# A recurrence with running maximum on one core: five steps of the last group, the start constants and the last store moved

## The chip, the core and the metric

The kernel runs on one core of a Trainium2 chip. The metric is device time in microseconds (us). Three timed runs of the kernel before took 290.93, 292.04 and 292.12 us (median 292.04). A further execution was profiled; it took 291.05 us, of which 289.3 us lie between its first and its last instruction (the span). Times in a trace are counted from the start of that span.

The engines are called as in the profile: PE (TensorE; PEld are its weight loads), DVE (VectorE), ACT (ScalarE), POOL (GpSimd) and SP (SyncE, which here only issues DMAs). A `q` behind a name (`POOLq`, `SPq`) marks what an engine's sequencer does, such as issuing a DMA or waiting.

## What is computed

For each of 16 batches and 256 channels a weighted mean runs over 2048 steps, with a numerator `aa`, a denominator `bb` and a running exponent `pp`:

```python
for t in range(seq_len):
    kk, vv = k[b, t, :], v[b, t, :]
    ww = u + kk
    qq = np.maximum(pp, ww)
    e1, e2 = np.exp(pp - qq), np.exp(ww - qq)
    output[b, t, :] = (e1 * aa + e2 * vv) / (e1 * bb + e2 + 1e-08)
    ww = pp - w + kk
    qq = np.maximum(ww, kk)
    e1, e2 = np.exp(ww - qq), np.exp(kk - qq)
    aa = e1 * aa + e2 * vv
    bb = e1 * bb + e2
    pp = qq
```

`k`, `v` and the output are 16 x 2048 x 256 in float32; `w` and `u` have 256 values each.

## The kernel before

Time is cut into 16 groups of 128 steps (`c` = 0 to 15), each of two halves of 64 steps, and the batches into 4 sets of four. A pair `n` = 4c + p (0 to 63) is one group for one set of batches: a tile of 128 steps x 4 batches x 256 channels for `k`, one for `v`, one for the output.

Each pair goes through these steps. Their short names are those of the plan in the code, and are used in the text:

- LK, LV load `k` and `v`, by SP for the first three pairs and by POOL after that (L108, L111, L115). RK rounds `k` for PE (`kr`, L194, DVE or POOL). CV casts `v` to bfloat16 (`vb`, L214, DVE for the first ten pairs).
- R and L put `u`, `w` and running sums of `k` into one of two PSUM tiles X0, X1 on PE (L201, L207), X takes the exponentials on ACT into the ring `EZR` (L210), and TV multiplies by `v` on DVE (L219). `u` and `w` reach PE through the tile WU, made by two operations on DVE (L175, L176) from the row tile WUf, which is cleared (L124) and then filled by two small DMAs (L122: `u` issued by POOL, `w` by ACT).
- S sums over the steps of the pair into the PSUM tile TOT on PE (L245).
- DEN forms the denominator in X0 or X1 on PE (L322), LN takes its logarithm on ACT (`rd<-X`, L330), INV takes exp of minus that on ACT (`rd<-rd`, L338). NUM forms the numerator on PE (L322, into the one tile `num`, or into X for the odd pairs of the last eight), MUL multiplies the two on DVE (`ot`, L350). There are two `rd` and eight `ot` buffers.
- ST stores the output by SP (L363 the first two batches; L356 a piece of 64 steps of the others). SQ stores the last piece: for pairs 52 to 63 by POOL (L356), before that by SP. For pair 63 INV and MUL are done in two halves.

Between the groups the state is carried on. After the last pair of group c: CS copies TOT to SBUF (DVE, L251), TU turns it on PE (L258), SL takes logarithms (ACT, L262), FR and OF make frames and offsets (DVE, L267 to L275), SW the weights from them (ACT, L281), CH runs two scans (DVE, L285, L288), SS spreads the result (DVE, L295), TK turns it back on PE (L302), BK copies it to the tile `cb` (DVE, L306). DEN and NUM of pairs 4c to 4c+3 read `cb` of group c, so the last four pairs, 60 to 63, need TK 15 and BK 15.

The order is written by a planner. Every step gets a place, a number in units of pairs, from the table P; steps are taken in order of place as soon as the steps that they follow and the buffers that they take are there, and each engine executes its instructions in that order. A table AT can set the place of a single step by name; it is empty before. The program ends (L480) when SP has waited for every store, each engine has drained, and a barrier led by POOL is through.

Ahead of the planned steps stands a start: memsets on DVE (WUf first), 26 multiplications by zero on PE that read the tile Z (L149), selects and iotas on POOL, and then on DVE nine memsets of state tiles (L231 to L236). The step `mats` (four small multiplications on DVE that make Id, IdN, S and SN, L182) has a place of -9.17 and follows directly.

```python
    for j in range(2):
        K(DVE.memset(CB_of[j].bitcast(F32), 0.0))
        K(DVE.memset(U_of[j][:, FR, :, 0:1], -BIG))
...
    step("mats", P["mats"], make_matrices)
    step("wu", P["wu"], make_rows)
```

Of the kernel before, what the change touches and what calls it, by code (L numbers as in the profile page):

```python
# [7 lines left out]
F32 = mybir.dt.float32  # L8
# [3 lines left out]
ACT = mybir.ActivationFunctionType  # L12
# [3 lines left out]
def kernel(  # L16
# [9 lines left out]
    K = tc.keep_in_program_order  # L26
    PE, DVE, SC, POOL, SP = nc.tensor, nc.vector, nc.scalar, nc.gpsimd, nc.sync
# [5 lines left out]
    D = 2 * Dm  # L33
    NP = 4 * NST
# [10 lines left out]
    RS = 2.0 ** -20  # L45
    CAP = 54.0
    BIG = 1e30
# [14 lines left out]
         "Z0": {"L": 1, "S": 3, "DEN": 0, "NUM": 6, "TK": 47, "TU": 17, "R": 12},  # L62
         "Z": {"DEN": 0, "L": 1, "NUM": 0, "TK": 4, "S": 0, "TU": 1, "R": 0}}

    AT = {}

    consts = ctx.enter_context(tc.tile_pool(name="consts", bufs=1))
    kpool = ctx.enter_context(tc.tile_pool(name="kpool", bufs=NK))
# [3 lines left out]
    rpool = ctx.enter_context(tc.tile_pool(name="rpool", bufs=NRD))  # L72
# [14 lines left out]
    def matrix(name, dt):  # L87
        return consts.tile([128, 128], dt, tag=name, name=name)
# [10 lines left out]
    def how(n):  # L99
        return "D" if n < BYSP else FIRST[n] if n < len(FIRST) else PLAN[n % len(PLAN)]  # L100
# [4 lines left out]
    def load_k(n):  # L105
        if how(n) != "C":
            KR[n] = raw(opool, "ot") if n < BYSP else raw(kppool, "kf")
            K((SP if n < BYSP else POOL).dma_start(out=KR[n], in_=rows_of(k, n)))  # L108
        else:
            KR[n] = kpool.tile([128, 4, Dm], F32R, tag="kr", name="kr")  # L110
            K(POOL.dma_start(out=KR[n], in_=rows_of(k, n)))  # L111
# [6 lines left out]
    WUf = rpool.tile([128, 2, D], F32, tag="rd", name="WUf")[:, 0, 0:Dm]  # L118
# [2 lines left out]
    def row_wu(queue, x, g):  # L121
        K(queue.dma_start(out=WUf[g::32, :], in_=bass.AP(tensor=x.tensor, offset=x.offset, ap=[[0, 4], list(x.ap[0])])))  # L122

    K(DVE.memset(WUf, 0.0))  # L124
    load_k(0)
    row_wu(POOL, u, 1)
    row_wu(SC, w, 0)
# [50 lines left out]
    mats = {name: matrix(name, BF16) for name in ("Id", "IdN", "S", "SN")}  # L178
# [11 lines left out]
    X = [psx.tile([128, 2, D], F32, tag=f"X{a}", name=f"X{a}") for a in range(2)]  # L190
# [31 lines left out]
    AS, D1, L1, A0, FR, BC, A2 = range(7)  # L222
    U_of = [consts.tile([128, 7, 32, 3], F32, tag=f"U{j}", name=f"U{j}") for j in range(2)]
    G_of = [consts.tile([128, 3, 32, 3], F32, tag=f"G{j}", name=f"G{j}") for j in range(2)]
    TB_of = [consts.tile([128, 2, 32, 3], F32, tag=f"TB{j}", name=f"TB{j}") for j in range(2)]
    CB_of = [consts.tile([128, 4, 128], BF16, tag=f"CB{j}", name=f"CB{j}") for j in range(2)]
    AB = consts.tile([128, 2, 32, 3], F32, tag="AB", name="AB")
    st = {}

    for j in range(2):  # L230
        K(DVE.memset(CB_of[j].bitcast(F32), 0.0))  # L231
        K(DVE.memset(U_of[j][:, FR, :, 0:1], -BIG))
        K(DVE.memset(G_of[j][:, :, :, 0:1], 0.0))
    K(DVE.memset(U_of[0][:, D1, :, 0:1], -100.0))
    K(DVE.memset(U_of[0][:, L1, :, 0:1], 0.0))
    K(DVE.memset(TB_of[0][:, :, :, 0:1], 0.0))  # L236

    def sums(n):
        c, p = divmod(n, 4)
# [70 lines left out]
    RD, NUM, OT = {}, {}, {}  # L310
# [14 lines left out]
    def den(n, a):  # L325
        apply(X[a], n, ("S", "Id"), 1)

    def log_den(n, a):
        rd = rpool.tile([128, 2, D], F32, tag="rd", name="rd")
        K(SC.activation(rd, X[a], ACT.Ln, scale=RS))  # L330
        RD[n] = rd

    def parts(n):
        return (slice(0, 1), slice(1, 2)) if n == NP - 1 else (slice(0, 2),)

    def inverse(n):
        for i in parts(n):
            K(SC.activation(RD[n][:, i], RD[n][:, i], ACT.Exp, scale=-1.0))  # L338

    def by_x(n):  # L340
        return n >= NP - XT and n % 2 == 1
# [11 lines left out]
    def piece(n, h, queue):  # L353
        c, p = divmod(n, 4)
        t0 = c * TC + HS * (1 - h)
        K(queue.dma_start(out=out[4 * p + 2:4 * p + 4, t0:t0 + HS, :].rearrange("n t d -> t n d"), in_=OT[n][HS * h:HS * h + HS, 2:4, :]))  # L356

    def shared(n):
        return n >= BYPOOL or BYQ[n % len(BYQ)] == "P" and n >= BYF
# [5 lines left out]
            piece(n, h, SP)  # L365

    def store_rest(n):
        piece(n, 1, POOL)


    ops, free = {}, {"K": NK, "KP": NKP, "V": NV, "N": 1, "RD": NRD, "OT": NOT, "VB": NVB}
# [1 line left out]
    def step(name, place, fn, args=(), after=(), take=None, give=(), mode=0):  # L373
        key = name if isinstance(name, str) else " ".join(map(str, name))
        ops[name] = dict(place=AT.get(key, place), fn=fn, args=args, after=list(after), take=take, give=give, mode=mode)

    for n in range(NP):
        c, j = divmod(n, 4)
        early = n < BYSP
        vb = "OT" if n < VOT else "V"  # L380
        put = lambda key: n + P[key][j]
        lead = SOON * max(0.0, 1 - n / UNTIL)
        lag = LAG - sum(n < x for x in LAGS)
        m = n + lag - lead
        tail = n >= NP - LAG
        place = lambda key: m + (P["TAIL"][key] + (n - NP + LAG) * P["TAIL"]["step"] if tail else P["OUT"][key][int(n + lag + 2) % 4])
        kb = "OT" if early else "KP" if how(n) != "C" else "K"
        if n:
            step(("LK", n), n + P["LK"], load_k, (n,), [("LK", n - 1)], kb)
        else:  # L390
            free["OT"] -= 1
        step(("LV", n), n + P["LV"], load_v, (n,), [("LV", n - 1)] + ([("LK", n)] if n else []), vb)
        if how(n) != "C":
            step(("RK", n), put("RK"), round_k, (n,), [("LK", n), ("RK", n - 1)], "K", [kb])
        for q in range(2):
            step(("R", q, n), n + P["R"][q], rows, (n, q), ["wu", ("R", 1 - q, n - 1 + q)], "X", mode=3)
            step(("L", q, n), n + P["L"][q], logs, (n, q), [("R", q, n), ("LK", n), ("RK", n), ("L", 1 - q, n - 1 + q)], None,
                 ["K"] if q else [], 1)
            step(("X", q, n), n + P["X"][q], exps, (n, q), [("L", q, n), ("NUM", n - RING), ("S", n - RING)], None, ["X"])
        step(("CV", n), put("CV"), cast_v, (n,), [("LV", n), ("CV", n - 1)], "VB", [vb])  # L400
        step(("TV", n), put("TV"), times_v, (n,), [("X", 1, n), ("CV", n), ("TV", n - 1)], None, ["VB"])
        step(("S", n), put("S"), sums, (n,), [("TV", n), ("S", n - 1)] + ([("CS", c - 1)] if j == 0 else []), mode=2)
        if j == 3:
            s = P["STATE"][0 if c == 0 else 2 if c == NST - 1 else 1]
            for i, (name, fn, *after) in enumerate((
                    ("CS", copy_sums, ("S", n)), ("TU", turn, ("CS", c), ("CH", c - 1)), ("SL", state_logs, ("TU", c)),
                    ("FR", state_frames, ("SL", c), ("SN", c - 1)), ("OF", state_offsets, ("FR", c)),
                    ("SW", state_weights, ("OF", c)), ("CH", state_chain, ("SW", c), ("KP", c - 1)),
                    ("SS", state_spread, ("CH", c)), ("TK", turn_back, ("SS", c), "mats"), ("BK", copy_back, ("TK", c)),
                    ("SN", state_next, ("OF", c)), ("KP", state_keep, ("CH", c)))):  # L410
                if not (name in ("SN", "KP") and c + 1 == NST):
                    step((name, c), n + s[i] - lead * SHARE, fn, (c,), after, mode=1)
        step(("DEN", n), place("DEN"), den, (n,), [("BK", c), ("DEN", n - 1), "mats"], "X", mode=3)
        step(("LN", n), place("LN"), log_den, (n,), [("DEN", n), ("INV", n - 1)], "RD", ["X"])
        step(("INV", n), place("INV"), inverse, (n,), [("LN", n)])
        step(("NUM", n), place("NUM"), num, (n,), [("BK", c), ("TV", n), ("NUM", n - 1), "mats"], "X" if by_x(n) else "N", mode=3)
        step(("MUL", n), place("MUL"), mult, (n,), [("NUM", n), ("INV", n), ("MUL", n - 1)], "OT", ["X" if by_x(n) else "N", "RD"])
        step(("ST", n), place("ST"), store, (n,), [("MUL", n), ("ST", n - 1)], None, [] if shared(n) else ["OT"])
        if shared(n):
            step(("SQ", n), place("SQ"), store_rest, (n,), [("ST", n)], None, ["OT"])  # L420
    step("mats", P["mats"], make_matrices)
    step("wu", P["wu"], make_rows)

    quiet = False
# [60 lines left out]
```

## Time and profile before

| | us or share |
|---|---|
| timed runs, median (lowest to highest) | 292.04 (290.93 to 292.12) |
| the profiled execution, its own time | 291.05 |
| span of the profiled execution | 289.3 |
| PE busy | 272.0 (94%) |
| ACT busy | 258.1 (89%) |
| DVE busy | 246.1 (85%) |
| POOL busy | 176.9 (61%) |
| moved by DMA | 101.21 MB, mean 350 GB/s |
| first useful matmul (L201) | 7.87 |
| last multiplication on DVE ends (L350) | 282.55 |
| last store issued (POOL, L356) | 282.84 |

Busy shares are an average over the start, a long middle of equal groups, and the tail. How long an engine was idle ahead of an instruction, and what ended the wait, stands in brackets behind a row of the timeline. Matmuls are pipelined and their ends are modelled, so the PE rows overlap. A wait for several events is put down to the one that came last by the profile.

### The profile page before, as it was taken

How to read it: one execution, taken by the hardware profiler on the slowest of the kernel's cores; microseconds unless marked ns; L12 is line 12 of the kernel's file. 1: busy time of each engine (PE TensorE's matmuls, PEld its weight loads, DVE VectorE, ACT ScalarE, POOL GpSimd, SP SyncE). 2: the span in 40 equal slices, each digit the busy share in tenths (PEclk: the TensorE clock that was granted, in tenths of full speed). 3: DMA queues.
4: the chain of work that ended last, by engine and by line, in shares of the span. 5: the costliest groups of instructions: out<-in, count | busy, mean ns of one | idle time of the engine just before them, and what ended most of it. 6: DMA issues, size and time to landing. Idle time of an engine off the chain costs nothing.

```text
span 289.3 us, 8057 instructions
## 1 busy us (share of the span) xinstructions
PE 272.0 (94%) x3263; PEld 139.5 (48%) x3263; DVE 246.1 (85%) x423; ACT 258.1 (89%) x290; POOL 176.9 (61%) x219
## 2 busy tenths in 40 slices
PE   7899999999999999999999999999999999997750
PEld 6445744444545455444545454554545455444330
DVE  6666889989898989899897979899898989797860
ACT  1587399999999999999999999999999999997890
POOL 7267367675767686675757686775757674422230
PEclk9999999999999999999999999999999999999995
DMA  7999999999999999999999999999999999896895
GB/s 229 351 347 347 348 343 337 382 328 392 386 393 380 371 387 377 393 383 392 391 381 382 385 385 388 392 365 397 391 391 382 389 363 390 294 247 180 221 265 147
DMA packets 58574, 101.21 MB, mean 350 GB/s; under 512 B 5152, under 2 KB 43560, under 8 KB 58536
## 3 DMA queue, kind: packets, MB, share of 16 engines
q0 software_dynamic: 21248, 65.55, 65.2%
q1 hardware_dynamic: 37280, 35.14, 36.3%
q8 instruction: 25, 0.41, 0.6%
q14 instruction: 13, 0.11, 0.1%
q10 hardware_dynamic: 8, 0.00, 0.0%
HBM read 67.12 MB, written 33.55 MB: 348 GB/s over the span
## 4 chain that ended last, share of the span: by engine, by line
PE 83%; DVE 4%; ACT 4%; issue 3%; POOL 1%; DMA 1%; POOLq 0%; SPq 0%; DVEq 0%
PE X L207 21%; PE X L322 15%; PE num L322 13%; PE X L201 12%; PE TURN L149 12%; PE TOT L245 7%; ACT EZR L210 2%; PE TOT L258 2%; DVE ot L350 1%; PE TURN L302 1%; POOL out_dram L356 1%; DMA out_dram<-ot 1%; ACT rd L330 1%; DVE EZR L219 1%; ACT rd L338 1%
## 5 line engine op out<-in xcount | busy, mean ns | idle before, releaser
L210 ACT ACTIVATE EZR<-X 128x1024 bf16<-128x1024 f32 x128 | 126.8, 1013 | 14.2 <-PE X L207 14.1
L214 POOL CAST vb<-vr 128x1024 bf16<-128x1024 f32 x54 | 56.3, 1042 | 69.7 <-DVE EZR L219 68.1
L219 DVE TENSOR_TENSOR EZR<-EZR,vb 128x2048 bf16<-128x2048 bf16 x64 | 77.8, 1218 | 0.4 <-ACT EZR L210 0.2
L350 DVE TENSOR_TENSOR ot<-num,rd 128x1024 f32<-128x1024 f32 x60 | 73.2, 1220 | 4.6 <-ACT rd L338 3.2
L338 ACT ACTIVATE rd<-rd 128x1024 f32<-128x1024 f32 (+1 forms) x65 | 67.9, 1046 | 2.0
L330 ACT ACTIVATE rd<-X 128x1024 f32<-128x1024 f32 x64 | 65.6, 1025 | 2.5 <-PE X L322 0.9
L149 PE MATMUL TURN<-Z 128*128 128x192 bf16 x319 | 55.7, 261 | 1.6 <-DVE Z L133 1.6
L201 PE MATMUL X<-WU,CO 64*64 64x512 bf16 x512 | 51.9, 390 | 1.1 <-DVE WU L176 0.9
L149 PEld LDWEIGHTS <-Z 128*128 128x128 bf16 x319 | 28.9, 101 | 48.9 <-issue 47.1
L115 POOL DMA_DIRECT2D vr<-in_v_dram x61 | 46.0, 753 | 6.5 <-DVE vb L214 6.5
L207 PE MATMUL X<-kr,NLE 128*128 128x512 f32 x128 | 45.6, 438 | 0.0
L207 PE MATMUL X<-kr,NLZ 128*128 128x512 f32 x128 | 45.5, 437 | 0.0
L108 POOL DMA_DIRECT2D kf<-in_k_dram x53 | 40.2, 758 | 0.0
L194 DVE CAST kr<-kf 128x1024 fp32r<-128x1024 f32 x39 | 30.6, 813 | 4.4 <-DMA kf<-in_k_dram 4.2
L201 PEld LDWEIGHTS <-CO 64*64 64x64 bf16 x512 | 15.7, 105 | 31.4 <-issue 26.4
L322 PE MATMUL X<-EZR,S 64*64 64x512 bf16 x256 | 26.2, 394 | 1.7 <-ACT rd L330 1.0
L322 PE MATMUL X<-cb,Id 64*64 64x512 bf16 x256 | 25.8, 376 | 0.0
L322 PE MATMUL X<-EZR,Id 64*64 64x512 bf16 x256 | 25.8, 376 | 0.0
L322 PE MATMUL num<-EZR,SN 64*64 64x512 bf16 x240 | 24.3, 386 | 1.1 <-DVE ot L350 1.1
L322 PE MATMUL num<-cb,IdN 64*64 64x512 bf16 x240 | 24.0, 376 | 0.0
L322 PE MATMUL num<-EZR,IdN 64*64 64x512 bf16 x240 | 23.9, 376 | 0.0
L245 PE MATMUL TOT<-EZR,OH 128*32 128x256 bf16 x512 | 23.4, 277 | 0.5 <-DVE EZR L219 0.5
(69 smaller groups left out, 270.0 us busy)
## 6 DMA issues: line engine op xcount, KB each, us to landing
vr<-in_v_dram POOLq DMA_DIRECT2D x61, 512.0 KB, 7.9
kf<-in_k_dram POOLq DMA_DIRECT2D x53, 512.0 KB, 8.8
out_dram<-ot SPq DMA_DIRECT2D x64, 256.0 KB, 10.2
out_dram<-ot SPq DMA_DIRECT2D x116, 128.0 KB, 10.1
kr<-in_k_dram POOLq DMA_DIRECT2D x8, 512.0 KB, 8.2
ot<-in_k_dram SPq DMA_DIRECT2D x3, 512.0 KB, 5.0
ot<-in_v_dram SPq DMA_DIRECT2D x3, 512.0 KB, 8.3
out_dram<-ot POOLq DMA_DIRECT2D x12, 128.0 KB, 3.3
```

Source lines behind the costliest of these rows:

```text
L115: K((SP if n < BYSP else POOL).dma_start(out=vr, in_=rows_of(v, n)))
L149: K(PE.matmul(TURN[:, 0:192], Z[:, 0:128], Z, start=first, stop=True, skip_group_check=True))
L201: K(PE.matmul(X[a][o:o + HS, i, :].rearrange("p (n d) -> p n d", n=2), CO[r:r + HS, q, :], WU[r:r + HS, :].unsqueeze(1).broadcast_to([HS, ...
L207: K(PE.matmul(X[a][:, i, :], (NLE, NLZ)[q], km[:, i, :], start=False, stop=True, skip_group_check=True))
L210: K(SC.activation(ez(n)[:, q, 1], X[a], ACT.Exp))
L214: K((DVE if n < EARLY else POOL).tensor_copy(vb, VR.pop(n)))
L219: K(DVE.tensor_mul(ez(n)[:, :, 0], ez(n)[:, :, 1], vb.unsqueeze(1).broadcast_to([128, 2, 2, D])))
L245: K(PE.matmul(t[32 * j:32 * j + 32, 0:256], OH[:, s:s + 32], ez(n)[:, 0, 1 - q, i, 256 * x:256 * x + 256], start=p == 0 and x == 0, stop=p ...
L322: K(PE.matmul(out_tile[o:o + HS, i, :], left, right, start=s == 0, stop=s == 2, tile_position=(r, o), skip_group_check=True))
L330: K(SC.activation(rd, X[a], ACT.Ln, scale=RS))
L338: K(SC.activation(RD[n][:, i], RD[n][:, i], ACT.Exp, scale=-1.0))
L350: K(DVE.tensor_mul(o.rearrange("p (i n) d -> p i (n d)", i=2)[:, i], NUM[n][:, i], RD[n][:, i]))
```

## The change

INV 55 is placed ahead of SL 15 and LN 56 of the last group; SW 15 is placed ahead of INV 56, where it stood behind LN 57. On DVE this puts CH 15 and SS 15 ahead of MUL 56, behind which CH stood before. On PE and SP no instruction changes its order. For pair 63 LN is split into two halves as INV was, in the order LN, INV, LN, INV. The last piece of pair 63 is stored by ACT instead of POOL. WUf is cleared by POOL instead of DVE. The nine memsets of state tiles become a step `zero`, which SL must follow; it and `mats` get the places 1.01 and 1.0, so on DVE the 13 operations come behind `vb` of pair 1 (L214) instead of ahead of the first `kr`.

```diff
-    AT = {}
+    AT = {"INV 55": 69.0, "SL 15": 69.1, "LN 56": 69.2, "SW 15": 75.7, "FR 15": 69.3}
...
-    K(DVE.memset(WUf, 0.0))
+    K(POOL.memset(WUf, 0.0))
     load_k(0)
     row_wu(POOL, u, 1)
     row_wu(SC, w, 0)
...
-    for j in range(2):
-        K(DVE.memset(CB_of[j].bitcast(F32), 0.0))
-        K(DVE.memset(U_of[j][:, FR, :, 0:1], -BIG))
-        K(DVE.memset(G_of[j][:, :, :, 0:1], 0.0))
-    K(DVE.memset(U_of[0][:, D1, :, 0:1], -100.0))
-    K(DVE.memset(U_of[0][:, L1, :, 0:1], 0.0))
-    K(DVE.memset(TB_of[0][:, :, :, 0:1], 0.0))
+    def start_states():
+        for j in range(2):
+            K(DVE.memset(CB_of[j].bitcast(F32), 0.0))
+            K(DVE.memset(U_of[j][:, FR, :, 0:1], -BIG))
+            K(DVE.memset(G_of[j][:, :, :, 0:1], 0.0))
+        K(DVE.memset(U_of[0][:, D1, :, 0:1], -100.0))
+        K(DVE.memset(U_of[0][:, L1, :, 0:1], 0.0))
+        K(DVE.memset(TB_of[0][:, :, :, 0:1], 0.0))
...
-    def log_den(n, a):
-        rd = rpool.tile([128, 2, D], F32, tag="rd", name="rd")
-        K(SC.activation(rd, X[a], ACT.Ln, scale=RS))
-        RD[n] = rd
-
     def parts(n):
         return (slice(0, 1), slice(1, 2)) if n == NP - 1 else (slice(0, 2),)

+    def log_den(n, a):
+        RD[n] = rpool.tile([128, 2, D], F32, tag="rd", name="rd")
+        for i in parts(n):
+            K(SC.activation(RD[n][:, i], X[a][:, i], ACT.Ln, scale=RS))
+            if i.stop == 1:
+                invert(n, i)
+
+    def invert(n, i):
+        K(SC.activation(RD[n][:, i], RD[n][:, i], ACT.Exp, scale=-1.0))
+
     def inverse(n):
-        for i in parts(n):
-            K(SC.activation(RD[n][:, i], RD[n][:, i], ACT.Exp, scale=-1.0))
+        invert(n, parts(n)[-1])
...
     def store_rest(n):
-        piece(n, 1, POOL)
+        piece(n, 1, POOL if n < NP - 1 else SC)
...
-                    ("CS", copy_sums, ("S", n)), ("TU", turn, ("CS", c), ("CH", c - 1)), ("SL", state_logs, ("TU", c)),
+                    ("CS", copy_sums, ("S", n)), ("TU", turn, ("CS", c), ("CH", c - 1)), ("SL", state_logs, ("TU", c), "zero"),
...
-    step("mats", P["mats"], make_matrices)
+    step("mats", 1.0, make_matrices)
+    step("zero", 1.01, start_states)
```

## What was expected before the run

> **What bounds the kernel now.** Times are us from the start of the span of the one profiled execution: 291.05 us, of which the span is 289.3. First the busy time of each engine by stage (columns: length, then busy us of PE, PEld, DVE, ACT, POOL, granted clock, DMA share, GB/s).
>
> ```profile
> 0.00:7.87 7.87, 5.35 (x38) 5.02 (x39) 5.54 (x38) 1.28 (x1) 6.25 (x20) 1.00 0.74 238
> 40.00:256.00 216.00, 215.66 (x2635) 106.66 (x2638) 197.41 (x320) 212.41 (x242) 147.94 (x169) 1.00 1.03 376
> 256.00:271.50 15.50, 12.57 (x197) 6.54 (x192) 13.77 (x26) 12.91 (x15) 3.85 (x7) 1.00 0.76 211
> 271.50:283.50 12.00, 6.59 (x108) 3.40 (x100) 7.17 (x7) 10.04 (x11) 3.79 (x7) 0.95 0.88 252
> 283.50:289.30 5.80, 0.00 (x0) 0.00 (x0) 0.00 (x0) 0.00 (x0) 0.00 (x0) 0.50 0.40 117
> ```
>
> From 40 to 256 PE is busy 215.66 of 216.00 us in an order that the change leaves alone: what starts earlier ends earlier by as much, and only the start, the tail and the closing 5.8 us can be shortened. Second, the timeline of the start:
>
> ```profile
> 4.59 0.27 DVE L231 MEMSET CB<- 128x256 f32 x1
> ...
> 6.22 0.68 DVE L194 CAST kr<-ot 128x1024 fp32r<-128x1024 f32 x1
> 6.83 0.47 DVE L175 CAST WU<-WUf 128x256 bf16<-128x256 f32 x1
> 7.33 0.48 DVE L176 SCALAR_TENSOR_TENSOR WU<-WU,low,WUf 128x256 bf16<-128x256 bf16 x1
> ```
>
> The first useful matmul (L201, 7.87) waits for WU, WU stands behind the first kr cast, and that behind 13 constants (4.59 to 6.22). The chain of waits runs through these rows. Third, the timeline of the tail, DVE, then ACT:
>
> ```profile
> 264.96 1.23 DVE L350 TENSOR_TENSOR ot<-num,rd 128x1024 f32<-128x1024 f32 x1
> 267.19 1.22 DVE L350 TENSOR_TENSOR ot<-num,rd 128x1024 f32<-128x1024 f32 x1 [1.00 <-DMA out_dram<-ot]
> 268.33 0.28 DVE L285 TENSOR_TENSOR TB<-TOT,G 128x128 f32<-128x128 f32 x1
> ```
>
> ```profile
> 263.47 0.28 ACT L262 ACTIVATE U<-TOT 128x128 f32<-128x128 f32 x1 [1.76 <-PE TOT L258]
> 263.65 1.05 ACT L338 ACTIVATE rd<-rd 128x1024 f32<-128x1024 f32 x1
> ...
> 267.51 0.36 ACT L281 ACTIVATE G<-U 128x192 f32<-128x192 f32 x1
> ...
> 271.54 1.02 ACT L330 ACTIVATE rd<-X 128x1024 f32<-128x1024 f32 x1 [0.74 <-PE X L322]
> ```
>
> ACT idles 1.76 us, then runs INV 55 (263.65), LN 56, INV 56, LN 57 and only then SW 15 (267.51); CH 15 (L285) follows on DVE at 268.33; PE waits 0.74 us for its result (L302 at 269.68), ACT 0.74 us (LN 59). The 1.00 put down to a DMA at 267.19 is not one: MUL 56 reuses the buffer of pair 48, whose last store was issued at 249.47 and at the median of 10.1 us landed by 260; num 56 on PE (266.24 to 267.08) came last. From 271.54 ACT goes back to back, 2.0 us a pair. Fourth, the program's last line:
>
> ```profile
> L480 SPq EVENT_SEMAPHORE  x11: 17/28/3230, 283.3 to 289.3; - x11
> L480 POOLq DRAIN  x3: 46/161/5381, 282.8 to 289.1; - x3
> L480 SPq DRAIN  x3: 7/7/7, 287.2 to 288.7; - x3
> ```
>
> SP, which waits for every store, is done at 287.2; POOL's drain lasts from 282.8 to 288.2, and the last 1.1 us begin behind it. POOL ends last, not the last store.
>
> **Start (WUf by POOL, constants later).** k of pair 0 is issued at 0.81 and lands 4.0 later, at 4.8; u is issued at 1.50 and lands 5.0 later, at 6.5. Without the constants kr runs from 4.85 to about 5.5, and WU waits for u. So WU can start at about 6.55 instead of 6.83, if u is issued no later. The memset of 128x256 on POOL has no row: at least 0.10 (POOL's 128x1 memsets), at most 1.04 (its cast of 128x1024); I take 0.1 + 1.04/4 = 0.36, near its 128x128 select (0.30). It can start where DVE's did (0.93), so u is issued at about 1.3, against 1.50, where POOL woke 0.3 after DVE's memset (1.20), as it does at its stores (280.92 to 281.20). At 1.04 u is issued at 2.0 and lands 0.5 later. The gain is 0.25, with ends of +0.45 and -0.25. The selects and iotas behind u on POOL, with the loads of pairs 3 and 4, move as u's issue does; their readers have more room than WU. PE's zeros start 0.27 sooner with Z.
>
> The 13 constants (1.64 from first to last) go between vb 1 and vb 2. By rows, less 0.25: vb 1 at 13.32, constants 13.93 to 15.57, vb 2 and TV 1 at 16.19, done 17.4. PE wants TV 1 in the second half of the sums that it starts at 17.80 - 0.25, so at 17.83: 0.4 us of cover. vb 3 (16.98 before, waiting for its load) comes at 17.33, TV 3 ends at 20.35, wanted at 22.5. Cost nothing; what the constants take beyond 0.4 us more is paid by PE in full. Bounds: 0 and 3.3 (last rival).
>
> **Tail (INV 55, SL 15, LN 56, SW 15, FR 15).** INV 55 moves into the idle 1.76 (261.7 to 262.8). SL 15 stays at 263.47, since it waits for PE; the offsets on DVE (263.79 to 265.03) and MUL 55 (264.96) stay. LN 56 follows when DEN 56 is done, 264.26 (264.60 before: 0.34 sooner). SW 15 comes 0.91 behind it, as it came behind LN 57: 265.17, done 265.5; its offsets are ready at 265.03. INV 56 follows at 265.42, LN 57 0.96 later at 266.38. So CH 15 stands directly behind MUL 55: 264.96 + 1.14 = 266.11, and SS 15 ends at 267.45 (269.63 before). PE is then the later: num 56 and DEN 58 end the same, num 57 (which needs LN 57, 266.38 + 1.06 = 267.44) starts at 267.54, zeros at 268.31, TK 15 at about 268.65 (269.68 before). num 58 and DEN 59 follow as before: DEN 59 at 269.67, ready for ACT 0.87 later, 270.54. ACT has a second limit: LN 58 needs the rd that MUL 56 frees. MUL 56 is now behind SS 15: 267.31 to 268.56; LN 58 268.62, INV 58 269.66, LN 59 at 270.61. Against 271.54 that is **0.93** sooner, and from there on ACT's 2.0 us a pair carry it. Bounds: nothing (if TK comes no earlier) and 1.2 (ACT alone, LN 59 at 270.35).
>
> **Last pair.** LN 63 is split. Its 1.04 becomes two steps of about 0.63 and 0.54 with INV between; the last INV ends 0.15 later, MUL's second half too. SP meanwhile is issuing (pieces of 62 until 281.96, main part of 63 until 282.60), so piece 0 moves from 282.70 by only 0.03. The earlier first half is worth nothing, for the same reason. Cost 0.05, bounds 0.2 either way.
>
> **End (last piece by ACT).** POOL's last store is now that of pair 62 (281.20 instead of 282.84), so the drain, 4.75 us behind the issue, ends 1.64 sooner, at 286.6, and SP's 287.2 is last. POOL reacts 0.28 later: 287.5 for 288.2, **0.7** gained, if ACT's piece lands with SP's (issued at 282.70, 4.1 to landing). ACT's issue waits for MUL 63 and nothing stands behind it on ACT. ACT has one issue to go by, w: 1.11 us against SP's 0.60. So bounds are 0.9 and 0.2. The row first: POOL's piece took 3.7 to land, SP's 4.1. The Trainium skill (DMA: Bandwidth & Descriptors, Issuing engines are not separate DMA queues) says that DMAs of all issuers share the same 16 DMA engines and that another issuer saves only sequencer time; the trace agrees. By that rule alone the edit would bring under 0.2, since no landing moves; the drain is a row the rule does not speak of.
>
> **Sum.** 0.25 + 0.93 - 0.05 + 0.7 = 1.8: 291.05 becomes 289.2. The three timed runs shown have a median of 292.04 (290.93 to 292.12); the four executions average 291.5, so I take **289.7**.
>
> **Rivals.**
> - *The end is not shortened* (drain bound to something else, or ACT's piece late): gain 1.1, **290.4**. For it: ACT's 1.11. Against: nothing else is issued by POOL. 0.16.
> - *u lands late*: POOL's memset held up until DVE's memsets end (2.16): u issued at 2.5, WU at 7.55, 0.7 lost for 0.25 gained; **290.6**. Against: POOL's casts take 1.04 to 1.05 beside a busy DVE. 0.09.
> - *The tail gains nothing*, since PE or an rd buffer holds TK 15 or LN 59 where they were: **290.6**. 0.08.
> - *The constants block DVE* (slower): they now lie beside POOL's load issues (13.49 to 15.35). In the rows of before, beside the issue at 5.27, the four multiplications took 0.18, 0.50, 0.44 and 0.21. If each waited out a whole issue (0.74 to 1.06), 3.7 us would come on, 0.4 covered: PE 3.3 late, **293.0**. It loses to the gains from 2.2 us on. Against: the four took 0.70 together. The Trainium skill (SBUF — State Buffer, Who interferes with whom) has it that a VectorE cast or tensor_scalar in a two-port mode and a GpSimd instruction lock each other out entirely; the 0.50 agrees, and by the rule the time would lie toward this rival. 0.05.
>
> **Numbers.** Forecast 0.62. The range 288.6 to 291.2 takes in the first three rivals and the 1.1 us between the runs. Faster by over 0.5% (1.46 us, about what a measurement of this kernel can tell from no change) 0.68, within 0.25, slower 0.07.
>
> **What would show it.** WU at about 6.6 and L201 at 7.6; no PE wait for TV 1 near 17.8; SW 15 between LN 56 and INV 56, TK 15 without a wait for CB, LN 59 0.9 us sooner relative to LN 55; POOL's drain over before SP's. Wrong if WU still follows late u, if PE waits near 17.8, or if the drain still ends last.

## The result and the profile after

| | median (lowest to highest), us | runs |
|---|---|---|
| before | 291.64 (290.93 to 292.12) | 9 |
| after | 289.53 (288.80 to 290.38) | 9 |

The ratio is 0.9928, 95% interval 0.9916 to 0.9940: 2.1 us faster, against 2.3 forecast from the median shown and 1.8 from the profiled execution. The profiled execution of the kernel after took 289.2 us, its span is 287.5 us (before: 291.05 and 289.3). In the closing table below one disturbed execution of a repeated kernel (827.9 us) is left out. In the code after the change, the lines of before are one further on from L231 to L322; LN is L335, INV L340, MUL L355, a piece of a store L361, the program's end L486.

**The start** in the kernel after, on DVE (columns: start, length, engine, line, operation, out<-in, count, idle time before it and what ended it):

```profile
5.07 0.71 DVE L194 CAST kr<-ot 128x1024 fp32r<-128x1024 f32 x1 [0.67 <-DMA ot<-in_k_dram]
5.96 0.29 DVE L175 CAST WU<-WUf 128x256 bf16<-128x256 f32 x1 [0.17 <-DMA WUf<-in_u_dram]
6.29 0.48 DVE L176 SCALAR_TENSOR_TENSOR WU<-WU,low,WUf 128x256 bf16<-128x256 bf16 x1
...
13.18 0.69 DVE L214 CAST vb<-ot 128x1024 bf16<-128x1024 f32 x1 [0.27 <-DMA ot<-in_v_dram]
13.79 0.41 DVE L182 TENSOR_SCALAR Id<-I 128x128 bf16<-128x128 f32 x1
...
15.48 0.11 DVE L237 MEMSET TB<- 128x64 f32 x1
16.25 0.69 DVE L214 CAST vb<-ot 128x1024 bf16<-128x1024 f32 x1 [0.66 <-DMA ot<-in_v_dram]
16.86 1.22 DVE L219 TENSOR_TENSOR EZR<-EZR,vb 128x2048 bf16<-128x2048 bf16 x1
```

WU now waits for its own data, not for constants, and the first L201 comes at 6.83, 1.04 sooner than before. But vb 2 (16.25) waits 0.66 for its load, TV 1 (16.86) stands behind it, and PE waits for TV 1 in the sums:

```profile
16.77 0.50 PE L246 MATMUL TOT<-EZR,OH 128*32 128x256 bf16 x10
18.13 0.40 PE L246 MATMUL TOT<-EZR,OH 128*32 128x256 bf16 x6 [0.86 <-DVE EZR L219]
```

In the kernel before the same sums ran through without a wait:

```profile
17.80 0.62 PE L245 MATMUL TOT<-EZR,OH 128*32 128x256 bf16 x16
18.35 0.41 PE L201 MATMUL X<-WU,CO 64*64 64x512 bf16 x4
```

The L201 behind the sums now comes at 18.46, so from here PE is 0.1 behind the kernel before. The whole 1.04 is gone in this execution.

**The tail** of the kernel after on ACT:

```profile
261.88 1.06 ACT L340 ACTIVATE rd<-rd 128x1024 f32<-128x1024 f32 x1
263.61 0.28 ACT L263 ACTIVATE U<-TOT 128x128 f32<-128x128 f32 x1 [0.67 <-PE TOT L259]
264.40 1.03 ACT L335 ACTIVATE rd<-X 128x1024 f32<-128x1024 f32 x1 [0.51 <-PE X L323]
265.32 0.36 ACT L282 ACTIVATE G<-U 128x192 f32<-128x192 f32 x1
...
268.74 1.03 ACT L335 ACTIVATE rd<-X 128x1024 f32<-128x1024 f32 x1
...
270.76 1.01 ACT L335 ACTIVATE rd<-X 128x1024 f32<-128x1024 f32 x1
```

INV 55 (261.88) fills the idle time, SW 15 (265.32) comes between LN 56 and INV 56, 2.19 sooner than before, and LN 59 starts at 270.76 instead of 271.54. LN 55 had started 0.14 later, so the tail itself gained 0.92. On DVE and then on PE, the last line being TK 15 in the kernel before:

```profile
265.08 1.22 DVE L355 TENSOR_TENSOR ot<-num,rd 128x1024 f32<-128x1024 f32 x1
266.21 0.28 DVE L286 TENSOR_TENSOR TB<-TOT,G 128x128 f32<-128x128 f32 x1
...
267.42 1.22 DVE L355 TENSOR_TENSOR ot<-num,rd 128x1024 f32<-128x1024 f32 x1
```

```profile
268.76 0.39 PE L303 MATMUL TURN<-Id,CB 128*128 128x128 bf16 x4
```

```profile
269.68 0.40 PE L302 MATMUL TURN<-Id,CB 128*128 128x128 bf16 x4 [0.74 <-DVE CB L295]
```

CH 15 (L286) stands directly behind MUL 55, and TK 15 (L303) no longer waits. LN 58 at 268.74 follows MUL 56 (267.42 + 1.22 = 268.64), the buffer limit that the prediction named.

**The end** of the kernel after, three lines of the program's last statement (columns: shortest/median/longest in ns, first start to last start):

```profile
L486 SPq EVENT_SEMAPHORE  x11: 17/28/28, 282.6 to 287.4; - x11
L486 POOLq DRAIN  x3: 51/249/5148, 280.4 to 287.2; - x3
L486 SPq DRAIN  x3: 7/7/7, 286.2 to 286.5; - x3
```

POOL's long drain, 280.4 + 5.15 = 285.5, is over before SP's last wait (286.2); before it ended at 288.2, 1.0 behind SP. From LN 63 to the end of the span (278.76 to 287.5, before 279.56 to 289.3) it is now 8.7 us instead of 9.8.

### The profile page after: what moved, and what is told of

It is laid out like the page before. It is cut to its first block, busy times and chain, and to the rows that moved or that the text cites. A ratio compares the mean times of both kernels' runs of the same rounds, so it can differ in the third digit from the quotient of the medians.

```text
span 287.5 us, 8058 instructions
## 1 busy us (share of the span) xinstructions
PE 271.6 (94%) x3263; PEld 139.2 (48%) x3263; DVE 246.9 (86%) x422; ACT 258.6 (90%) x291; POOL 176.4 (61%) x219
## 4 chain that ended last, share of the span: by engine, by line
PE 81%; ACT 6%; DMA 4%; DVE 4%; issue 2%; SPq 1%; DVEq 0%; ACTq 0%
PE X L207 20%; PE X L323 15%; PE num L323 12%; PE X L201 12%; PE TURN L149 11%; PE TOT L246 7%; DMA ot<-in_v_dram 4%; ACT rd L335 3%; PE TOT L259 2%; DVE ot L355 2%; ACT rd L340 2%; DVE EZR L219 1%; ACT EZR L210 1%; PE TURN L303 1%; SPq L115 1%
## 5 line engine op out<-in xcount | busy, mean ns | idle before, releaser
L214 POOL CAST vb<-vr 128x1024 bf16<-128x1024 f32 x54 | 56.4, 1044 | 69.3 <-DVE EZR L219 67.5
L355 DVE TENSOR_TENSOR ot<-num,rd 128x1024 f32<-128x1024 f32 x60 | 73.3, 1221 | 3.9 <-ACT rd L340 3.6
L340 ACT ACTIVATE rd<-rd 128x1024 f32<-128x1024 f32 (+1 forms) x65 | 68.0, 1046 | 2.0
L335 ACT ACTIVATE rd<-X 128x1024 f32<-128x1024 f32 (+1 forms) x65 | 65.8, 1012 | 2.3 <-PE X L323 0.7
L201 PE MATMUL X<-WU,CO 64*64 64x512 bf16 x512 | 51.9, 390 | 0.9 <-DVE WU L176 0.6
L207 PE MATMUL X<-kr,NLE 128*128 128x512 f32 x128 | 45.6, 438 | 0.0
L207 PE MATMUL X<-kr,NLZ 128*128 128x512 f32 x128 | 45.5, 437 | 0.0
L194 DVE CAST kr<-kf 128x1024 fp32r<-128x1024 f32 x39 | 31.6, 839 | 4.0 <-DMA kf<-in_k_dram 4.0
L201 PEld LDWEIGHTS <-CO 64*64 64x64 bf16 x512 | 15.7, 105 | 31.1 <-issue 26.3
```

What stands on the lines that cost most here:

```text
L201: K(PE.matmul(X[a][o:o + HS, i, :].rearrange("p (n d) -> p n d", n=2), CO[r:r + HS, q, :], WU[r:r + HS, :].unsqueeze(1).broadcast_to([HS, ...
L207: K(PE.matmul(X[a][:, i, :], (NLE, NLZ)[q], km[:, i, :], start=False, stop=True, skip_group_check=True))
L214: K((DVE if n < EARLY else POOL).tensor_copy(vb, VR.pop(n)))
L335: K(SC.activation(RD[n][:, i], X[a][:, i], ACT.Ln, scale=RS))
L355: K(DVE.tensor_mul(o.rearrange("p (i n) d -> p i (n d)", i=2)[:, i], NUM[n][:, i], RD[n][:, i]))
```

## The experiments

The theory after the result: the tail is worth 0.9, the end 0.7 to 1.1, the start nothing, because TV 1 is late.

### The tail alone, the end alone, the start alone

The kernel before with the table AT of the change, `tail_alone`:

> The kernel before with the five places of the last group alone. Theory (the order of the tail is worth what the profile after shows): LN 59 starts 0.92 us sooner relative to LN 55, and the time falls by 0.9 us. Rival (the rows of the tail only hide a wait that comes back in the last four pairs, or the gain of the profile after came from the end alone): under 0.3 us.

Ratio 0.9971 (0.9957 to 0.9985), so 0.4 to 1.25 us faster, middle 0.85. In the profile LN 59 starts at 270.54, 0.93 sooner as counted from LN 55. (The span of this one execution is only 0.1 shorter than before, since its last stores landed late: POOL's 4.6 after its issue, against 3.7.) The rival of a gain under 0.3 falls.

The kernel before with one line changed, `end_alone`:

```diff
-        piece(n, 1, POOL)
+        piece(n, 1, POOL if n < NP - 1 else SC)
```

> The kernel before with the last piece issued by ACT and nothing else. Theory (POOL's drain, about 4.7 us behind its last issue, was what ended last): POOL's drain is over before SP's waits are, and the time falls by 0.7 to 1.1 us. Rival (issuers share the DMA engines, so another issuer saves only the time of its sequencer): within 0.2 us, since no landing moves by more. Rival two (ACT's issue is dear, 1.11 us for w): the piece lands later, gain under 0.4 us.

Ratio 0.9962 (0.9947 to 0.9977): 0.7 to 1.5 us, middle 1.1, for one store moved to another queue. Both rivals fall; ACT's issue took 0.75, not the 1.11 of w. The profile, in which LN 63 to the end took 8.9, shows what a drain waits for:

```profile
L480 POOLq DRAIN  x3: 51/93/4953, 281.5 to 288.4; - x3
L480 SPq DRAIN  x3: 7/7/7, 287.6 to 287.9; - x3
```

The drain begins at 281.46 and ends at 286.42. POOL's last store landed at 284.82, 1.60 sooner. The distance is 1.60 to 1.64 in all thirteen profiles, whatever the time from issue to landing was: before 286.56 and 288.20, `tail_alone` 286.41 and 288.05, `quiet_split` (below) 287.68 and 289.31. SP's wait ends 0.3 to 0.4 behind the last landing of all: before 286.79 and 287.18, after 285.82 and 286.20. So a last store from POOL is closed 1.6 us after it lands, one from SP or ACT 0.3 to 0.4 after.

The kernel before with the start's edits alone (WUf by POOL, `mats` and `zero` behind vb 1), `start_alone`:

> The kernel before with the start's edits alone: WUf cleared by POOL, the four matrices and nine state memsets behind vb 1. By the prediction: 0.25 us faster. By the profile after: the first L201 comes 1.0 us sooner, TV 1 comes late behind the constants and vb 2, PE waits for it near 18, and the time is within 0.2 us of the kernel before.

Ratio 0.998 (0.9965 to 0.9996): 0.1 to 1.0 us faster, middle 0.6. That is above the expectation from the profile after (within 0.2), though the interval reaches into it; the 0.25 of the prediction lies inside. The profiled execution, one of the slower (291.72, where the runs lie between 290.81 and 292.43), tells a third thing. v of pair 2 landed at 15.21 here (after: 16.16, before: 14.26), TV 1 was nearly in time, and PE was 0.76 ahead at pair 4. At pair 63 it was 0.70 *behind* the kernel before. Aligning the two rows of PE instructions shows where: 0.25 near 23, 0.23 near 46, and then three steps at 91, 156 and 237 that each begin with an idle PE and cost 0.33 in the end. The middle one, DVE, POOL and PE of `start_alone`:

```profile
153.24 1.40 DVE L194 CAST kr<-kf 128x1024 fp32r<-128x1024 f32 x1 [0.90 <-DMA kf<-in_k_dram]
154.57 1.21 DVE L351 TENSOR_TENSOR ot<-num,rd 128x1024 f32<-128x1024 f32 x1
```

```profile
153.06 1.04 POOL L194 CAST kr<-kf 128x1024 fp32r<-128x1024 f32 x1
```

```profile
155.03 0.41 PE L323 MATMUL X<-cb,Id 64*64 64x512 bf16 x4
155.83 0.41 PE L323 MATMUL num<-EZR,SN 64*64 64x512 bf16 x4 [0.38 <-DVE ot L351]
```

And the same place in the kernel before, DVE and POOL:

```profile
152.89 0.73 DVE L194 CAST kr<-kf 128x1024 fp32r<-128x1024 f32 x1 [0.58 <-DMA kf<-in_k_dram]
153.67 1.22 DVE L350 TENSOR_TENSOR ot<-num,rd 128x1024 f32<-128x1024 f32 x1
```

```profile
153.02 1.50 POOL L194 CAST kr<-kf 128x1024 fp32r<-128x1024 f32 x1
```

Two roundings of k meet here, one on DVE and one on POOL. Whoever begins first takes its usual time (DVE 0.73, POOL 1.04); the other is stretched (POOL to 1.50, DVE to 1.40). DVE's waits for a load of k. Where that load lands 0.35 later, DVE loses, MUL behind it starts 0.90 later, and PE waits 0.38 for the one `num` tile. The Trainium skill (SBUF — State Buffer, Who interferes with whom) says that a VectorE cast in a two-port mode and a GpSimd instruction share one pair of ports, which whoever comes first holds for the whole instruction. These rows agree in the order, and nearly in the size: the second ends 0.54 (DVE) or 0.90 (POOL) behind the first, 0.14 less than it takes alone. That the casts here run in such a mode no run shows by itself. A stretched rounding does not always cost: the kernel after has several of 1.38 to 1.40 (152.4 and 168.5 among them) with no PE wait. There the load came earlier, and DVE began beside POOL's cast of v, which comes ahead of POOL's rounding.

### TV 1 ahead

The kernel after, with `"CV 2": 2.8` in AT and `mats` and `zero` made to follow TV 1, `tv1_ahead`:

> The kernel after with two moves on DVE: TV 1 directly behind vb 1, then the 13 constants, then vb 2. Theory (the start's 1.0 us is lost because TV 1 stands behind the constants and behind vb 2, which waits for its load): TV 1 runs from 13.8 to 15.0, PE's wait of 0.86 us near 18 goes, and the time falls by 0.5 to 0.9 us against the kernel after, about 3 us against the kernel before. Rival (the late loads of v set the pace behind it): PE waits as long for TV 2 or TV 3 instead, and the time is within 0.2 us of the kernel after (-2.1 us).

Median 289.43 (after: 289.53); ratio to before 0.9923 (0.9904 to 0.9943). The rival's number, and the first half of the theory: TV 1 ran from 13.38, PE's wait near 18 was gone, and PE was 0.97 ahead at pair 4. It then lost 0.37 near 23 (0.2 of it a wait for a load of k), 0.28 near 46, and twice 0.33 to late roundings (123 and 156); at pair 63 it was 0.32 behind. So TV 1 alone is not what keeps the start's gain from the end.

### The rounding behind the multiplication

One number in the kernel before puts the rounding of each group behind MUL, which waits for ACT there anyway, `rounding_behind`:

```diff
-         "RK": [-2.85, -1.165, -3.305, -1.485]
+         "RK": [-1.9, -1.165, -3.305, -1.485]
```

> The kernel before with one move on DVE in each group: the rounding of k for the first pair of the next group but one comes behind the multiplication of the group's last pair, instead of ahead of it. Theory (a rounding whose load lands after POOL's own rounding has begun is stretched from 0.7 to 1.4-1.55 us, the multiplication behind it is late, and PE waits 0.38 us for num; how many groups are hit differs from run to run): no such stretched row ahead of a multiplication, no PE wait for num in the middle, the median falls from 291.8 to about 291.0, and the spread of the runs (1.9 us) shrinks to about 1 us. Rival (the spread comes from elsewhere): median and spread as before.

Ratio 0.9964 (0.9952 to 0.9976): median 290.59. The runs lie between 290.39 and 290.69, those of the kernel before beside them between 290.74 and 292.08. The theory holds, and with more than it claimed: the spread shrinks from 1.3 to 0.3 us (to 0.45 over 13 runs with those of `rounding_again` below), so most of the scatter of this one kernel was late roundings. DVE, then POOL, at the same place:

```profile
153.66 1.23 DVE L350 TENSOR_TENSOR ot<-num,rd 128x1024 f32<-128x1024 f32 x1 [1.35 <-ACT rd L338]
154.80 0.68 DVE L194 CAST kr<-kf 128x1024 fp32r<-128x1024 f32 x1
```

```profile
153.02 1.04 POOL L194 CAST kr<-kf 128x1024 fp32r<-128x1024 f32 x1
```

Neither rounding is stretched, and MUL beside POOL's cast takes its usual 1.23. The other profiles say the same. With the rounding behind (six profiles) none of POOL's 14 roundings is stretched and PE never waits for `num` between 40 and 256; in the kernel before 12 of the 14 take 1.50. With the rounding ahead, PE waits there for 0.38 not at all (before, `tail_alone`, after), once (`end_alone`), twice (`tv1_ahead`) or three times (`start_alone`, `last_by_sp`). At 0.33 kept of each that makes up to 1.0 us between executions. `end_alone` has such a wait without an early start, so whether an early start brings more of them is open.

The same line in the kernel after, `after_rounding_behind`, and in the kernel with TV 1 ahead, `tv1_rounding_behind`:

> The kernel after with the same one move on DVE. Theory: the start's gain is no longer eaten by the late roundings; median 288.9 (after: 289.5), lowest near 288.4. Rival: 289.5, unchanged.

> The kernel after with TV 1 directly behind vb 1, the 13 constants behind TV 1, and the rounding behind the multiplication in every group. Theory: of the 0.98 us that the first L201 is ahead, 0.35 to 0.6 still go in the first three groups where PE waits for loads of k, and the rest, 0.33, is kept to the tail, where the kernel with TV 1 ahead alone lost 0.33 twice: 0.3 to 0.7 under that kernel's 289.4, so 288.8. Rival (loads are the second limit through the whole middle): PE waits for k itself instead, 289.4.

Medians 288.60 (288.25 to 289.50) and 288.71 (288.36 to 289.77); ratios to before 0.9901 (0.9885 to 0.9916) and 0.9907 (0.9889 to 0.9925). The first is the best kernel of the study, 0.9 under the kernel after. In its profile PE is 1.01 ahead at first, 0.65 behind TV 1 (near 17.7), 0.45 from 23 on, and still 0.47 at pair 63: nothing more is lost in the middle. With TV 1 ahead PE is 0.99 ahead, then 0.59 (23), 0.29 to 0.42 (45 to 46.5), and 0.36 at pair 63. Either way some 0.4 of the 1.0 passes the first three groups. Near 23 it is a load of k: L207 begins 0.04 to 0.05 behind its landing in both and in `tv1_ahead` and `start_alone` (landings 22.84 to 22.99). In the kernel before that L207 began at 23.48, so with such landings only 0.45 to 0.6 can pass, however early the start is. What takes the rest near 46 stays open.

### The last piece by SP

The kernel after, with SP instead of ACT in `store_rest`, `last_by_sp`:

> The kernel after with the last piece issued by SP, behind its other stores, instead of ACT. If the end was gained because POOL's drain is no longer last, and not because ACT's piece lands early, all of it but SP's later issue is kept: SP issues the piece at about 282.5 instead of ACT's 281.9, so the end comes 0.6 us later, 290.1. If it was ACT's issue that made the gain: 290.6 (the whole 1.1 lost).

Median 289.51 (289.20 to 289.98), as after; ratio to before 0.9929 (0.9915 to 0.9942). That the gain is ACT's falls. Its profile has POOL's drain out of the way too, and SP last:

```profile
L486 POOLq DRAIN  x3: 51/241/4960, 280.7 to 287.6; - x3
L486 SPq DRAIN  x3: 7/7/7, 286.7 to 287.0; - x3
```

From LN 63 (279.10) to the end of the span it takes 8.8, after 8.7: SP issued the piece at 282.89 and it landed at 286.33. The 0.6 expected for the later issue doesn't show in the medians, and hardly in the landing: behind LN 63 the piece was issued 0.65 later and the last landing came 0.17 later. PE lost time to three late roundings in this execution, so its LN 63 is not to be compared with that of the kernel after.

### The small parts on the quiet base

With the rounding behind the multiplication the base is quiet enough to look for parts of a few tenths. The base again, `rounding_again`:

> The kernel of the run with the rounding behind, once more, as the quiet base of the three runs beside it: 290.6, spread under 0.5 us.

Median 290.55, lowest 290.34. With LN 63 split, `quiet_split`:

> The quiet base (rounding behind) with LN 63 in two halves alone. By the prediction's term +0.05; by the row of the kernel after (the last half of MUL ends 0.12 later behind LN 63) +0.12, since POOL's last store and its drain follow that half here; rival (the earlier first half lets SP store sooner): -0.1.

Median 290.89 (lowest 290.73, where 12 of the 13 runs of the base lie below that): 0.3 slower, more than any side expected. The profile has MUL's last half end 3.11 after the start of LN 63, against 2.99, so 0.12 of it is shown. Its profiled stores landed late (4.8 after issue, against 3.5), which the timed runs cannot tell; the rest stays open.

The start's edits, `quiet_start`, and the first of them, `quiet_wuf`:

> The quiet base with the start's edits alone (WUf by POOL, the 13 constants behind vb 1). If the roundings ate the start's gain: the first L201 comes 1.0 us sooner, PE loses 0.35 to TV 1 near 17.7 and 0.2 waiting for k near 23, and 0.4 us is kept: 290.2. If the loads of the middle take it all: 290.6.

> The quiet base with WUf cleared by POOL alone, the constants left where they were. u lands 0.6 us sooner, but WU still stands behind the first rounding of k and that behind the 13 constants: L201 moves by what DVE's missing memset frees, at most 0.27; time within 0.3 of the base. If instead u's landing was what L201 waited for, 0.6 sooner.

`quiet_start`: median 290.34 (290.14 to 290.74), 0.2 under the base, whose runs it overlaps, so this gain is not clear of noise. L201 came 0.77 sooner, and PE kept 0.64 of it to pair 63; TV 1 cost PE 0.1. The time fell by less than that: in the profiles, POOL's last piece was issued 0.63 sooner and landed 0.46 sooner. `quiet_wuf`: median 290.71, no gain; u landed at 6.20, but WU stood behind the rounding of k and that behind the 13 constants, so L201 came 0.09 sooner, as expected. If the start gains here, it comes from the constants' move, or needs both edits; the constants alone were not run.

Moving the rounding does not make every kernel quiet: the runs of `quiet_wuf` go from 290.60 to 292.96 (four of 12 above 291.6), those of `quiet_split` spread by 1.1, of `after_rounding_behind` by 1.25, of `tv1_rounding_behind` by 1.4. What scatters them is not shown.

| kernel | median, us | ratio to before (95%) |
|---|---|---|
| tail alone | 290.76 | 0.9971 (0.9957 to 0.9985) |
| end alone | 290.67 | 0.9962 (0.9947 to 0.9977) |
| start alone | 291.28 | 0.9980 (0.9965 to 0.9996) |
| after | 289.53 | 0.9928 (0.9916 to 0.9940) |
| TV 1 ahead | 289.43 | 0.9923 (0.9904 to 0.9943) |
| last piece by SP | 289.51 | 0.9929 (0.9915 to 0.9942) |
| before, rounding behind | 290.59 | 0.9964 (0.9952 to 0.9976) |
| the same again | 290.55 | 0.9963 (0.9950 to 0.9976) |
| that, LN 63 split | 290.89 | 0.9981 (0.9970 to 0.9992) |
| that, start's edits | 290.34 | 0.9957 (0.9942 to 0.9972) |
| that, WUf by POOL | 290.71 | 0.9984 (0.9968 to 1.0001) |
| after, rounding behind | 288.60 | 0.9901 (0.9885 to 0.9916) |
| that, TV 1 ahead | 288.71 | 0.9907 (0.9889 to 0.9925) |

Taken singly, the tail (0.85), the end (1.1), the start (0.6) and the split on its own base (0.3 lost) add up to 2.2, against 2.1 for the whole change.

## Why the prediction came out right

The time was right, 289.53 for 289.7, with two of its terms off in opposite directions: in the profiles the end with the last pair gave 1.06 for the 0.65 of the sum, and the start lost 0.14 by LN 55 where 0.25 was to be gained. That these cancel is luck.

- **Tail, 0.93.** Right in size and in every step: 0.92 in the profile, 0.85 (0.4 to 1.25) alone. The buffer of MUL 56, not ACT or PE, set LN 58, as forecast.
- **End, 0.7.** The mechanism was right (POOL's drain ended last, not the last store) and the size too small: 1.06 in the profile, the last pair's cost included, and 1.1 (0.7 to 1.5) alone. The mis-sized term is POOL's reaction behind SP, taken as 0.28: from SP's last wait to the end of the span it took 1.27, against 1.13 behind POOL's drain before, so it cost 0.14. Landings moved too, the last from 7.23 to 7.06 behind LN 63, which the prediction had left where it was. The drain was priced from its issue (4.75); it goes by the landing, plus 1.6. ACT's issue, feared at 1.11, took 0.73. The price by the rule of the Trainium skill (DMA: Bandwidth & Descriptors, Issuing engines are not separate DMA queues), under 0.2, did not come out; the rule speaks of moving data, and what was saved here was a wait behind the data.
- **Last pair, 0.05.** Mis-sized too: 0.12 in the profile, 0.3 in the timed runs on the quiet base, where the rest stays open.
- **Start, 0.25.** Its first half was too careful: POOL's memset took 0.31 (0.36 forecast) and u landed 4.5 behind its issue instead of 5.0, and the two operations that make WU took 0.81 instead of 0.98, so L201 came 1.04 sooner, not 0.25. The step that failed is "Cost nothing" for the constants, with 0.4 us of cover, and PE's wait near 17.8 was one of the prediction's own signs of being wrong. The cover was worked out with a gain of 0.25: with 1.04, PE wants TV 1 at 17.04 and not at 17.83, so TV 1 would have been 0.36 late even at the forecast 17.4 (`after_rounding_behind`, where it ended at 17.33, lost 0.34). On top, vb 2's load was held at 14.26. It landed at 16.16, the latest of all profiles, so TV 1 ended at 18.08 and PE waited 0.86. The 13 constants themselves took 1.80 against 1.64; the slower rival did not come.
- **"What starts earlier ends earlier by as much."** Failed as well. In `start_alone` PE entered the middle 0.76 ahead and left it 0.70 behind, with its order unchanged. A PE that is 99.8% busy (215.66 of 216.00) in one execution says nothing on what is just behind it: here loads of k that land within 0.4 us of their latest time. The sign was in the same profile: the prediction read POOL's casts as 1.04 to 1.05 beside a busy DVE, which holds for the 54 casts of v, while 12 of the 14 of k took 1.50. Where no rounding is late, the sentence holds: the 0.45 of `after_rounding_behind` at 23 is 0.47 at pair 63, and the kernel after keeps its 0.1.

That a small gain of the start was forecast and a small one measured (0.1 to 1.0 alone) is partly chance as well: more was gained at L201 and more was lost behind it.

## What to carry to other kernels

At the end of a program, look which engine's drain ends last, not which store: here a single last store moved off POOL was worth as much as a whole reordering of the tail. Ahead of trusting a gain at the start, follow it through the middle: list the loads that arrive just in time, and where two engines' casts can meet, let the one that waits for a load stand behind work that waits anyway. And when the runs of one kernel scatter by more than the edits are worth, search for the cause first: with one cause gone the runs of the kernel before lay within 0.45 us instead of 1.2 to 1.9, and a part of 0.3 could be seen.

## What was not expected of the hardware

- POOL's drain ends 1.60 to 1.64 us behind the landing of its last store (thirteen profiles, landings 3.3 to 4.8 us after issue); SP's wait for the last store, its own or ACT's, ends 0.3 to 0.4 behind the landing.
- A cast of 128x1024 on DVE and one on POOL do not share: 0.73 beside 1.50, or 1.40 beside 1.04, by which began first. Landings that differ by 0.35 us decide it; the runs of the kernel before differ by 1.2 to 1.9 us, and by 0.45 where the two casts do not meet.
- Where DVE clears WUf (five profiles), v of pair 2 landed at 14.26 to 14.75; where POOL does (eight), at 14.07 to 16.16, in six of them at 15.2 or later. POOL issues u 0.08 sooner there, and SP's issue of v of pair 0 beside it takes 0.72 to 0.77 us instead of 0.51. That the one causes the other was not shown.
